# Layer B's sample unit: two heads of 64 rows handled one by one, or above each other in 128 rows

## The chip, the cores and the metric

The kernel runs on one core of a Trainium2 chip. The metric is the device time of one execution in microseconds (us). The core has a matrix engine (TensorE, in the profile PE; its weight loads are PEld), a vector engine (VectorE, DVE), an engine for pointwise functions (ScalarE, ACT), a general one (GpSimd, POOL) and an engine that here only issues transfers (SyncE, SP). Each engine works through its own list of instructions in order and waits on semaphores of the others. TensorE writes to an accumulator memory, PSUM; the other data lie in SBUF, 128 rows (partitions) wide.

## What is computed

One step of a two-layer streaming encoder in float32: 2048 prompt tokens and 64 sample tokens, width 1024, 16 heads of 64 in layer B. Each layer is a gated attention block with a residual. Layer B's band is the own chunk of 64 frames and eight chunks before; the 64 sample tokens see a cache of 256 keys and themselves, so 320 keys, and no mask.

```python
def project(x, norm_g, w_in, q_g, k_g, n_heads, n_kv):
    p = rms_norm(x, norm_g) @ w_in
    q, k, v, gate = jnp.split(p, ...)
    return rms_norm(q, q_g), rms_norm(k, k_g), v, gate      # per head

# attend, layer B: no sinks
s = einsum('bqkgd,bskd->bkgqs', q, k) * dh ** -0.5 + bias
o = einsum('bkgqs,bskd->bqkgd', softmax(s), v)
# layer
y = x + (o * silu(gate)) @ w_out
```

The last rows of keys and values are outputs too.

## The kernel before

Float32 accuracy is made from a fast 32-bit matmul form: every operand is split into a high part and a low part, and a product is the sum of two or three matmuls. Probabilities are split the same way (ph and pl, line 1159), and keys and values carry their low parts in the other half of their rows or columns (KA, KB for the two heads of a prompt pair, KSA, KSB for the sample; VT and VS for values).

Layer B works in eight head pairs (hp). In each it goes through nine units: seven of 256 prompt tokens, then the sample unit of 64 tokens (u == NU), then the eighth prompt unit (order, L220). For each unit there are two kinds of work.

The first is the projection, the "filler" (class Filler, L614): generators that yield after every k-step of a projection, so that it can be cut into slices. Its accumulator pj has two buffers. For the sample tokens high and low parts stand beside each other as 128 columns of the stationary operand, so the accumulator has the sum in two halves of rows, which evacuate (L489) puts together, with ACT for rows 64 to 127 and DVE adding rows 0 to 63. Normalising heads (head_norm, L513), gates (gate), splitting weights and similar jobs go to a background queue (Background, L229): each job has a cost estimate, and each call of share (L272) runs jobs from the head of the queue until max(1.8, a quarter of the queue's cost) is spent. Urgent jobs stand ahead of the others. What share runs is tied, on each engine, behind the last attention instruction there (anchor, L245 and L257 to L265).

The second is attention, in functions that the loop of pipeline (L1201) calls:

- queries (L1044): transposes queries and keys of a unit into the PSUM tile tp, ACT scales the high parts out of it, and two background jobs (low, L1067, cost 1.0 each, urgent) make the low parts from the same tile on DVE, the last of them for KB at L1073. tp has one buffer.
- scores (L1082): score matmuls into sb (L1112, L1113), bias and row minimum on DVE (L1116), exponential and row sum on ACT (L1120), reciprocal, gate times reciprocal on POOL (L1130).
- values (L1137): transposes the probabilities (L596 is the helper that issues every transpose), splits them into ph and pl.
- outputs (L1165): the value product, keys by head width, with the values as stationary operand and the transposed probabilities as moving one (L1190, L1191); for the second head of a pair also the transpose of the gate into tp and finish_pairs (L978), which adds the high and the low half, multiplies with the gate and stores.

A prompt unit has four steps (two heads by two tiles), the sample unit two (its heads). A step of pipeline is: scores, a share, projection up to the first goal, values of the step before, a share, outputs that have come due, projection up to the second goal. queries of the next unit stand at the end of the second step of a prompt unit (QY = 1) and of the first step of the sample unit (QS = 0). TensorE's order is the program's order; on the other engines a scheduler orders the instructions by readiness, within the ties named above. SP issues loads and stores in one queue.

Of the kernel before, what the change touches and what calls it, by code (L numbers as in the profile page):

```python
# [15 lines left out]
P = 128  # L16
# [31 lines left out]
QS = 0  # L48
# [3 lines left out]
def hybrid_encoder_kernel(  # L52
# [296 lines left out]
    def load_act(src, o, T, squares=False, joint=False, lead=None, cache=None, cached=False):  # L349
# [42 lines left out]
        def square(c):  # L392
            def fn():
                s2 = t("res", [P, 2 * OT], 2)[:, : 2 * T].rearrange("p (k s) -> p k s", k=2)
                sq = nc.scalar.activation(s2, raws[c], AF.Square)
                if lead is not None and c > 0:
                    behind(sq.ins, held["wh"])
                part = t("sqr", [P, 2 * T if joint else T], 2)
                nc.vector.tensor_tensor(part[:, :T], s2[:, 0], s2[:, 1], op=ALU.add)
                if x.sum:  # L400
                    nc.vector.tensor_tensor(x.sum[0][:, :T], x.sum[0][:, :T], part[:, :T], op=ALU.add)
                else:
                    x.sum.append(part)
                if joint and c == 3:
                    nc.vector.tensor_copy(x.sum[0][:, T:], x.sum[0][:, :T])
                fetch()
            return fn
# [104 lines left out]

    def head_norm(n, src):  # L513
# [36 lines left out]
    def store_kv(layer, n, kn, v, kdst, vdst):  # L550
        def fn():
            ko = t("ko", [P, 2 * HD], 1)
            nc.gpsimd.tensor_tensor(ko[:n], kn, kgr[:n, layer, :], op=ALU.mult)
            store(kdst, ko[:n])
            store(vdst, v)

        return bg.put(0.1, fn)
# [41 lines left out]

    Q2 = [const([P, 512], f"q2_{i}", F32R) for i in range(2)]  # L600
# [4 lines left out]

    for q in Q2:
        zero(q[64:128])

# [51 lines left out]
    def layer_a():  # L660
# [4 lines left out]
        def add_unit(qd, place, unit):  # L665
# [30 lines left out]
            def take_kv(it, ps):  # L696
                tt, t0, n = it.tile
                last = u == NU
                it.kv = pr = evacuate(0, tt, n, ps, 256, 0)
                kn, v = pr[:n, 0:128], pr[:n, 128:256]  # L700
                split_v(n, v, VS[:, 1] if last else VT[:, tt])
                it.knorm = head_norm(n, kn)
                if last:
                    it.knorm.append(store_kv(0, n, kn, v, ka_s[64:128, :], va_s[64:128, :]))
                elif tt == NT - 1:
                    it.knorm.append(store_kv(0, n, kn, v, ka_p, va_p))
# [283 lines left out]
    def layer_b():  # L990
# [4 lines left out]
        def add_unit(hp, unit):  # L995
# [18 lines left out]
            def gen():  # L1014
# [3 lines left out]
                for e, (tt, t0, n) in enumerate(tiles):  # L1018
                    out = []
                    c = yield from project((tt, t0, n), xc, st.w[hp], 512, out)  # L1020
                    pr = evacuate(1, tt, n, out[0], 512, P, it.gate[:, e])
                    it.prs.append(pr)
                    v, kn = pr[:n, 256:384], pr[:n, 128:256]
                    split_v(n, v, VS[:, 2] if last else VT[:, tt])
# [3 lines left out]
                    if last:  # L1028
                        it.todo.append(store_kv(1, n, kn, v, kb_s[192:256, cols], vb_s[192:256, cols]))
                    elif tt >= NT - 4:  # L1030
                        o = (tt - (NT - 4)) * P
                        it.todo.append(store_kv(1, n, kn, v, kb_p[o : o + P, cols], vb_p[o : o + P, cols]))
# [11 lines left out]
        def queries(it):  # L1044
# [7 lines left out]
            for pr, (tt, t0, n) in zip(it.prs, tiles):  # L1052
                for j in range(2):
                    transpose(tp[:, j * T + t0 : j * T + t0 + n], pr[:n, j * P : (j + 1) * P])
            it.q1 = q1 = t("q1", [P, 2, UT], 2, F32R)
            it.q2 = q2 = low_queries().rearrange("p (h s) -> p h s", h=2)
            if u == NU:
                kd = [a[:, CB : CB + TS] for a in (KSA, KSB)]
            else:
                kd = [a[:, u * UT : (u + 1) * UT] for a in (KA, KB)]  # L1060
            qt = [tp[r, 0:T] for r in halves]
            kt = [tp[r, T : 2 * T] for r in halves]
            for hh, rows in enumerate(halves):
                nc.scalar.activation(q1[rows, hh, :T], qt[hh], AF.Identity, scale=qsc[rows, 1:2])
                nc.scalar.activation(kd[hh][rows], kt[hh], AF.Identity, scale=gk[rows])

            def low(hh, rows):  # L1067
                def fn():
                    nc.vector.scalar_tensor_tensor(
                        q2[rows, hh, :T], qt[hh], qsc[rows, 1:2], q1[rows, hh, :T].bitcast(F32),  # L1070
# [6 lines left out]
                    nc.vector.tensor_copy(q1[halves[1 - hh], hh, :T], q1[rows, hh, :T].bitcast(F32))  # L1077
# [4 lines left out]
        def scores(it, i, h):  # L1082
# [4 lines left out]
            bias = st.bias[hp][h]  # L1087
            last = u == NU
            tt, t0, n = tiles[i]
            if i == 0 and h == 0:  # L1090
# [5 lines left out]
                it.base = 0 if last else max(tt - 4, 0)  # L1096
            if last:
                K, k0, nk = (KSA, KSB)[h], 0, CB + TS
                near, b0 = P, 256
            else:  # L1100
                kt0 = max(tt - 4, 0)
                K, k0, nk = (KA, KB)[h], kt0 * P, (tt - kt0 + 1) * P
                near, b0 = max(nk - 256, 0), 640 - nk
            S = psum_b("sb", 1024, 2)
            rows = halves[h]
            o = 512 - near
            for c0, c1 in ((0, near), (near, nk)):
                if c0 == c1:
                    continue
                kk = K[:, k0 + c0 : k0 + c1]  # L1110
                dst = S[:n, o + c0 : o + c1]
                nc.tensor.matmul(dst, it.q1[:, h, t0 : t0 + n], kk, start=True, stop=False)  # L1112
                nc.tensor.matmul(dst, it.q2[:, h, t0 : t0 + n], kk, start=False, stop=True)  # L1113
            nmh = it.nm[:n, 2 * i + h : 2 * i + h + 1]
            it.p[i, h] = p = t("p", [P, 640], 3)
            mi = nc.vector.tensor_tensor_reduce(  # L1116
                out=p[:n, :nk], in0=S[:n, o : o + nk], in1=bias[:n, b0 : b0 + nk],
                op0=ALU.add, op1=ALU.min, scale=1.0, scalar=3e38, accum_out=nmh,
            )
            ex = nc.scalar.activation(  # L1120
                p[:n, :nk], p[:n, :nk], AF.Exp,
                scale=-1.0, bias=nmh, accum_out=it.sm[:n, 2 * i + h : 2 * i + h + 1],
            )
            bg.anchor(mi, ex)
            if i == len(tiles) - 1 and h == 1:
                w = 2 * len(tiles)
                nc.vector.reciprocal(it.sm[:n, :w], it.sm[:n, :w])
                it.G = G = t("G", [P, 256])
                for e in range(len(tiles)):
# [7 lines left out]
        def values(it, i, h):  # L1137
            u, T, tiles = it.unit
            last = u == NU
# [4 lines left out]
            if last:  # L1144
                sizes, kb = [P, P, TS], 0
            else:
                kt0 = max(tt - 4, 0)
                sizes, kb = [P] * (tt - kt0 + 1), kt0 - it.base
            PT = psum_b("sb", 1024, 2)
            PTv = PT.rearrange("p (c x) -> p c x", x=P)  # L1150
            for c, kn in enumerate(sizes):
                transpose(PTv[:kn, c, :n], it.p[i, h][:n, c * P : c * P + kn])
            full = sum(kn == P for kn in sizes)
            groups = [(0, full, P)]
            if last:
                groups.append((2, 1, TS))
            for c, m, kn in groups:
                bg.anchor(*split_to(
                    it.ph[h][:kn, kb + c : kb + c + m, t0 : t0 + n],
                    it.pl[h][:kn, kb + c : kb + c + m, t0 : t0 + n],  # L1160
                    PTv[:kn, c : c + m, :n],
                ))
            it.sizes = sizes

        def outputs(it, h):  # L1165
            u, T, tiles = it.unit
            last = u == NU
            n = tiles[0][2]
            sizes = it.sizes
            if h == 0:  # L1170
                it.O = psum("o", 512, 1)
            else:
# [3 lines left out]
                gt = gate_t(GT[:, :T].rearrange("p (j s) -> p j s", j=1), T)  # L1176
            mm = []
            if last:
                for c, kn in enumerate(sizes):
                    mm.append((VS[:kn, c, h], c, kn, 0, TS))  # L1180
            else:
                ta, tb = tiles[0][0], tiles[1][0]
                for kt in range(max(tb - 4, 0), ta + 1):
                    mm.append((VT[:, kt, h], kt - it.base, P, 0, UT))
                if ta >= 4:
                    mm.append((VT[:, ta - 4, h], ta - 4 - it.base, P, 0, P))
                mm.append((VT[:, tb, h], tb - it.base, P, P, UT))
            for x, (vt, c, kn, q0, q1_) in enumerate(mm):
                dst = it.O[:, h * T + q0 : h * T + q1_]
                nc.tensor.matmul(dst, vt, it.ph[h][:kn, c, q0:q1_], start=x == 0, stop=False)  # L1190
                nc.tensor.matmul(dst, vt, it.pl[h][:kn, c, q0:q1_], start=False, stop=x == len(mm) - 1)  # L1191
# [9 lines left out]
        def pipeline():  # L1201
# [8 lines left out]
            prev = pend = None  # L1210
            for x, it in enumerate(its):
                heads = [(i, h) for h in range(2) for i in range(len(it.unit[2]))]
                c0 = filler.done
                end, near = c0 + (PACE_B if len(heads) == 4 else PACE_S) * len(heads), 1e9
                if x + 2 < len(its):
                    near = its[x + 2].mark
                    if len(its[x + 1].unit[2]) + len(its[x + 2].unit[2]) < 4:
# [6 lines left out]
                for y, (i, h) in enumerate(heads):  # L1224
# [14 lines left out]
                    if y == (QY if len(heads) == 4 else QS) and x + 1 < len(its):  # L1239
# [4 lines left out]
            filler.to(filler.done + 2.6)  # L1244
            if pend is not None:
                outputs(*pend)
            filler.to(filler.done + 2.6)
            outputs(prev[0], prev[2])
# [210 lines left out]
```

## Time and profile before

| | |
|---|---|
| median of 3 runs | 2306.82 us (2306.8 to 2310.43) |
| the profiled execution's own time | 2309.3 us |
| its span, first to last instruction | 2307.5 us |
| mean granted TensorE clock | 0.998 |
| TensorE busy | 2264.3 us, 98% of the span |
| DVE, ACT, POOL busy | 1562.1, 1435.4, 843.2 us |
| DMA | 379.37 MB, mean 164 GB/s |

The profile is one execution on the chip, taken by the hardware's profiler. The span is its time from the first instruction to the last. L12 is a line of the kernel file; "o<-ph,VS" says that the instruction writes tile o from tiles ph and VS. "128\*64 64x64" beside a matmul gives the stationary operand (rows by columns) and the moving one. "[0.47 <-DVE KB L1073]" says that the engine stood idle for 0.47 us and that the DVE instruction of line 1073 released it. A matmul's length includes its way through the array and overlaps the next one; the distance between two starts is what it costs a busy TensorE.

### The profile page before, as it was taken

Reading aid. Unit: us, or ns where it says so; the run is one execution under the profiler, and the core shown is the slowest. Engines: PE = TensorE matmul, PEld = TensorE weight load, DVE = VectorE, ACT = ScalarE, POOL = GpSimd, SP = SyncE. Lnnn points to the kernel's source line nnn. Section 1 sums busy time; section 2 is a strip of 40 time slices with the busy share of each in tenths; the row PEclk is TensorE's granted clock in tenths of the full one; section 3 lists DMA queues with packets and bytes.
Section 4 is the critical chain, followed back from the end, with each engine's and each line's share of the span. In section 5 each row is a group of like instructions: output and inputs, shape, how many; then the busy total and the mean of one; then the engine's idle time right before and its main releaser. Section 6 shows DMA issues by size and latency. Waiting matters only on the chain.

```text
span 2307.5 us, 42459 instructions
## 1 busy us (share of the span) xinstructions
PE 2264.3 (98%) x13981; PEld 1983.6 (86%) x13981; DVE 1562.1 (68%) x5226; ACT 1435.4 (62%) x3640; POOL 843.2 (37%) x1186
## 2 busy tenths in 40 slices
PE   7999999999999999999999999999999999999999
PEld 6787888888889997888888888888888888888999
DVE  6779988888784446766766767767767677676211
ACT  6778777777774435766656656656656566565321
POOL 5554533333254446432222222222222222224443
PEclk9999999999999999999999999999999999999999
DMA  8846446754446777454444544544445445443665
GB/s 264 261 145 208 162 139 196 229 177 143 150 128 191 215 210 272 156 175 151 138 146 125 157 143 120 158 146 133 145 134 161 127 117 173 125 126 108 194 184 147
DMA packets 232125, 379.37 MB, mean 164 GB/s; under 512 B 24720, under 2 KB 163360, under 8 KB 231872
## 3 DMA queue, kind: packets, MB, share of 16 engines
q1 hardware_dynamic: 231904, 376.65, 53.5%
q8 instruction: 110, 1.80, 0.3%
q14 instruction: 111, 0.91, 0.1%
HBM read 296.13 MB, written 82.08 MB: 164 GB/s over the span
## 4 chain that ended last, share of the span: by engine, by line
PE 82%; DVE 6%; DMA 4%; ACT 4%; issue 2%; POOL 1%; SPq 1%; POOLq 0%; ACTq 0%; DVEq 0%
PE pj L480 13%; PE pj L482 13%; PE pj L481 13%; PE pj L1313 5%; PE pj L1314 5%; PE sb L596 5%; PE pj L1315 5%; PE o L1191 3%; PE o L1190 3%; PE tp L596 3%; PE sb L1112 3%; PE sb L1113 3%; PE sa L596 2%; DMA xraw<-in_x_rows_dram 1%; PE sa L877 1%
## 5 line engine op out<-in xcount | busy, mean ns | idle before, releaser
L480 PE MATMUL pj<-wh,xx 128*128 128x512 f32 (+1 forms) x1648 | 668.3, 406 | 5.3 <-ACT pb L503 4.6
L482 PE MATMUL pj<-wh,xx 128*128 128x512 f32 (+1 forms) x1648 | 638.1, 387 | 0.0
L481 PE MATMUL pj<-wl,xx 128*128 128x512 f32 (+1 forms) x1648 | 635.2, 385 | 0.0
L482 PEld LDWEIGHTS pj<-wh,xx 128*128 128x128 f32 x1648 | 310.8, 189 | 67.2
L480 PEld LDWEIGHTS pj<-wh,xx 128*128 128x128 f32 x1648 | 312.1, 189 | 45.7 <-ACT pb L503 5.3
L481 PEld LDWEIGHTS pj<-wl,xx 128*128 128x128 f32 x1648 | 312.9, 190 | 38.3 <-DVE wl L313 0.2
L384 POOL TENSOR_TENSOR xx<-xraw,xx 128x528 fp32r<-128x528 f32 (+1 forms) x200 | 265.2, 1342 | 200.9 <-ACT xx L383 192.7
L527 POOL TENSOR_TENSOR f<-f,mhalf 128x4 f32<-128x4 f32 (+3 forms) x221 | 227.8, 1031 | 228.4 <-DVE f L523 214.2
L1120 ACT ACTIVATE p<-p,nm 128x640 f32<-128x640 f32 (+5 forms) x272 | 204.3, 751 | 165.9 <-DVE nm L1116 164.1
L1313 PE MATMUL pj<-xx,wh 128*128 128x264 f32 x1024 | 294.0, 287 | 1.6 <-DVE res L1318 1.6
L1314 PE MATMUL pj<-xx,wh 128*128 128x264 f32 x1024 | 291.3, 284 | 0.0
L1315 PE MATMUL pj<-xx,wl 128*128 128x264 f32 x1024 | 289.9, 283 | 0.0
L1116 DVE CUSTOM_DVE_ANT_0 p<-sb,BT 128x640 f32<-128x640 f32 (+5 forms) x272 | 196.8, 724 | 120.1 <-PE sb L1113 116.5
L569 DVE TENSOR_TENSOR pl<-sb,ph 128x640 fp32r<-128x640 f32 (+5 forms) x288 | 196.8, 683 | 117.9 <-ACT ph L568 115.5
L568 ACT CAST ph<-sb 128x640 fp32r<-128x640 f32 (+5 forms) x288 | 167.2, 580 | 128.2 <-PE sb L596 119.9
L986 POOL TENSOR_TENSOR o<-gt,o 128x256 f32<-128x256 f32 (+2 forms) x140 | 107.1, 765 | 374.4 <-issue 156.8
L383 ACT CAST xx<-xraw 128x528 fp32r<-128x528 f32 (+1 forms) x200 | 122.4, 627 | 194.2 <-PE pj L1315 96.9
L1313 PEld LDWEIGHTS pj<-xx,wh 128*128 128x128 f32 x1024 | 192.8, 188 | 2.6 <-DVE res L1318 2.0
L523 DVE CUSTOM_DVE_ANT_0 sq<-pa 128x64 f32<-128x64 f32 (+1 forms) x850 | 171.5, 255 | 34.2 <-ACT pa L503 32.1
L1314 PEld LDWEIGHTS pj<-xx,wh 128*128 128x128 f32 x1024 | 192.5, 188 | 0.2
L1315 PEld LDWEIGHTS pj<-xx,wl 128*128 128x128 f32 x1024 | 192.6, 188 | 0.0
L1318 DVE TENSOR_TENSOR res<-pj,res 128x264 f32<-128x264 f32 x128 | 55.1, 431 | 200.6 <-PE pj L1315 195.6
(196 smaller groups left out, 4810.8 us busy)
## 6 DMA issues: line engine op xcount, KB each, us to landing
xx<-xsb SPq DMA_DIRECT2D x224, 512.0 KB, 4.3
xx<-xsa SPq DMA_DIRECT2D x88, 512.0 KB, 4.8
xraw<-oga SPq DMA_DIRECT2D x64, 264.0 KB, 3.6
xraw<-ogb SPq DMA_DIRECT2D x64, 264.0 KB, 3.3
xsa<-xx SPq DMA_DIRECT2D x32, 512.0 KB, 4.5
wraw<-in_w_in_b_dram SPq DMA_DIRECT2D x64, 256.0 KB, 3.5
xsb<-xx SPq DMA_DIRECT2D x32, 512.0 KB, 4.1
xraw<-in_x_dram SPq DMA_DIRECT2D x40, 256.0 KB, 4.4
```

The costliest lines, as they stand in the source:

```text
L384: nc.gpsimd.tensor_tensor(xl, rv, xh.bitcast(F32), op=ALU.subtract)
L480: nc.tensor.matmul(ps[:n, :C], xh, wh, start=k == 0, stop=False)
L481: nc.tensor.matmul(ps[:n, :C], xh, wl, start=False, stop=False)
L482: nc.tensor.matmul(ps[:n, :C], xl, wh, start=False, stop=k == KC - 1)
L527: nc.gpsimd.tensor_tensor(fv, fv, mhalf[:n, :H], op=ALU.pow)
L569: b = nc.vector.tensor_tensor(dst_lo, src, dst_hi.bitcast(F32), op=ALU.subtract)
L596: nc.tensor.transpose(out, in_, ident[:n, :n])
L1116: mi = nc.vector.tensor_tensor_reduce(out=p[:n, :nk], in0=S[:n, o : o + nk], in1=bias[:n, b0 : b0 + nk], op0=ALU.add, op1=ALU.min, scale=1 ...
L1120: ex = nc.scalar.activation(p[:n, :nk], p[:n, :nk], AF.Exp, scale=-1.0, bias=nmh, accum_out=it.sm[:n, 2 * i + h : 2 * i + h + 1],)
L1313: nc.tensor.matmul(ps[:, :OT], wh, oh, start=k == 0, stop=False)
L1314: nc.tensor.matmul(ps[:, :OT], wh, ol, start=False, stop=False)
L1315: nc.tensor.matmul(ps[:, :OT], wl, oh, start=False, stop=k == KC - 1)
```

## The change

The sample unit of layer B is handled in 128 rows, one head in the upper and one in the lower 64.

- evacuate_sample puts queries of both heads in the upper rows and keys in the lower rows of one 128 x 128 block, values beside them, and the gate with head 0 in the upper and head 1 in the lower rows: five pieces on ACT and five on DVE instead of two and two.
- One transpose brings queries and keys into tp. The queries go into QS, a constant tile of four 128 x 128 blocks (high and low of each head) that is zero outside its head's columns, so that four matmuls add up both heads' scores above each other in 128 rows.
- Bias and minimum stay two DVE instructions (one for each head's rows), the exponential is one of 128 rows. The columns 320 to 383 of the probabilities are zeroed on POOL, and rows 64 to 127 of the last value tile once at the start.
- Three transposes of 128 x 128 and one pair of splits turn the probabilities.
- sample_outputs takes the probabilities as stationary operand and the values of both heads, high and low, as 256 moving columns: six matmuls. The result has tokens in rows; high and low are added, the gate is multiplied without being transposed.
- sample_turned, one step later, transposes the result into tp, scales it by one half on ACT and stores it.
- The sample unit has one step in place of two. Its call of queries for the next unit stands ahead of the step's second goal. What values makes due is kept in a list, todo, of which each step takes one: outputs of the prompt unit before, then sample_outputs, then sample_turned, in the first, second and third step of the eighth prompt unit.
- In layer A, square's partial sums move from the tag sqr, which goes, to the tags G and o1.

```diff
-                part = t("sqr", [P, 2 * T if joint else T], 2)
+                part = t("o1" if x.sum else "G", [P, 256])
...
+    def evacuate_sample(tt, ps, g):
+        a = t("pa", [P, 384], 4)
+        lo, hi = halves
+        pieces = [
+            (a[lo, 0:128], 0), (a[hi, 0:128], 128), (a[lo, 256:384], 256),
+            (g[lo, 0:HD], 384), (g[hi, 0:HD], 384 + HD),
+        ]
+        sc = rr[1][:, tt : tt + 1]
+        for d, c in pieces:
+            nc.scalar.activation(d, ps[hi, c : c + d.shape[1]], AF.Identity, scale=sc[hi])
+        for d, c in pieces:
+            nc.vector.scalar_tensor_tensor(
+                d, ps[lo, c : c + d.shape[1]], sc[lo], d, op0=ALU.mult, op1=ALU.add
+            )
+        return a
...
+    QS = const([P, 4, P], "QS", F32R)
+    zero(QS)
+    zero(VS[64:128, 2])
...
+                    if last:
+                        pr = evacuate_sample(tt, out[0], it.gate[:, e])
+                        it.prs.append(pr)
+                        v, kn = pr[:n, 256:384], pr[n:, 0:128]
+                        split_v(n, v, VS[:, 2])
+                        it.todo += head_norm(P, pr[:, 0:128]) + gate(P, it.gate[:, e, 0:HD])
...
             if u == NU:
+                transpose(tp[:, 0:P], it.prs[0][:, 0:P])
                 kd = [a[:, CB : CB + TS] for a in (KSA, KSB)]
+                q1, q2 = ([QS[:, 2 * e + hh, hh * T : hh * T + T] for hh in range(2)] for e in range(2))
...
+            if u == NU:
+                n, nk, o, w = P, CB + TS, 0, 1
+                nc.gpsimd.memset(p[:, nk : 3 * P], 0.0)
+                for e in range(4):
+                    nc.tensor.matmul(
+                        S[:, :nk], QS[:, 2 * (e % 2) + e // 2], (KSA, KSB)[e // 2], start=e == 0, stop=e == 3
+                    )
+                soft = [(r, st.bias[hp][e][r, b0 : b0 + nk], 0) for e, (r, b0) in enumerate(zip(halves, (256, 320)))]
...
+        def then(it, i, h):
+            if it.unit[0] == NU:
+                return [lambda: sample_outputs(it), lambda: sample_turned(it)]
+            if i == len(it.unit[2]) - 1:
+                return [lambda: outputs(it, h)]
+            return []
+
+        def sample_outputs(it):
+            O = psum("o", 512, 1)
+            for c in range(3):
+                vs = VS[:, c].rearrange("p h d -> p (h d)")
+                nc.tensor.matmul(O[:, 0:256], it.ph[0][:, c, 0:P], vs, start=c == 0, stop=False)
+                nc.tensor.matmul(O[:, 0:256], it.pl[0][:, c, 0:P], vs, start=False, stop=c == 2)
+            it.o = o = t("o1", [P, 256])[:, 0:HD]
+            for hh, r in enumerate(halves):
+                nc.scalar.copy(o[r], O[r, hh * P : hh * P + HD])
+            for hh, r in enumerate(halves):
+                nc.vector.tensor_tensor(o[r], O[r, hh * P + HD : (hh + 1) * P], o[r], op=ALU.add)
+            nc.gpsimd.tensor_tensor(o, it.G[:, 0:HD], o, op=ALU.mult)
+
+        def sample_turned(it):
+            tp = psum("tp", 512, 1)
+            transpose(tp[0:HD, 0:P], it.o)
+            o = t("o1", [P, 256])[:, 0:TS]
+            for hh, r in enumerate(halves):
+                nc.scalar.activation(o[r], tp[0:HD, hh * TS : (hh + 1) * TS], AF.Identity, scale=0.5)
+            store(og[1][:, it.hp, SEQ:TOK], o)
...
+                sample = it.unit[0] == NU
+                heads = [(0, 0)] if sample else [(i, h) for h in range(2) for i in range(2)]
...
-                    nxt = None
+                    nxt = todo.pop(0) if todo else None
                     if prev is not None:
                         values(*prev)
                         bg.share(BL, BP_)
-                        if prev[1] == len(prev[0].unit[2]) - 1:
-                            nxt = prev[0], prev[2]
+                        todo += then(*prev)
                     prev = it, i, h
-                    if pend is not None:
-                        outputs(*pend)
-                    pend = nxt
+                    if nxt is not None:
+                        nxt()
+                    if sample and x + 1 < len(its):
+                        queries(its[x + 1])
+                        near = 1e9
                     goal(2 * y + 2)
```

More of the change, by code (lines that the diff above doesn't have):

```diff
@@ L1076, in fn @@
                     )
[L1077 removed]
+                    nc.vector.tensor_copy(q1[hh][halves[1 - hh]], q1[hh][rows].bitcast(F32))
                 return fn
@@ L1100, in scores @@
             else:
                 kt0 = max(tt - 4, 0)
-                K, k0, nk = (KA, KB)[h], kt0 * P, (tt - kt0 + 1) * P
+                K, k0, nk, w = (KA, KB)[h], kt0 * P, (tt - kt0 + 1) * P, 4
                 near, b0 = max(nk - 256, 0), 640 - nk
[L1104 to L1113, printed above, removed]
@@ L1153, in values @@
[L1153 to L1163, printed above, removed]
+            for c in range(m):
+                transpose(PTv[:, c, :n], it.p[i, h][:n, c * P : (c + 1) * P])
@@ L1243, in pipeline @@
             values(*prev)
[L1244 to L1248, printed above, removed]
+            todo += then(*prev)
+            while todo:
+                filler.to(filler.done + 2.6)
+                todo.pop(0)()
         return pipeline
```

129 lines of the change are left out of this document (68 added, 61 removed).

## The prediction

> **What bounds the kernel now.** I read the page first, then a table of layer B's stretch, then the list of what TensorE waited for, then the timeline of one sample unit.
>
> ```profile
> span 2307.5 us, 42459 instructions
> PE 2264.3 (98%) x13981; PEld 1983.6 (86%) x13981; DVE 1562.1 (68%) x5226; ACT 1435.4 (62%) x3640; POOL 843.2 (37%) x1186
> PE 82%; DVE 6%; DMA 4%; ACT 4%; issue 2%; POOL 1%; SPq 1%; POOLq 0%; ACTq 0%; DVEq 0%
> ```
>
> ```profile
> 1010.00:2133.00 1123.00, 1114.40 (x6596) 959.34 (x6595) 777.25 (x2630) 701.11 (x1773) 312.18 (x487) 1.00 0.46 138
> ```
>
> ```profile
> PE sb L596 <- DVE nm L1116: 4.0, 7, 0.8
> PE tp L596 <- DVE KB L1073: 1.9, 2, 1.4
> ```
>
> TensorE is busy 98% of the span and 82% of the chain of waits. In layer B's stretch (columns: length, then busy time of PE, weight load, DVE, ACT, POOL, then the granted clock) it is busy 1114.4 of 1123 us while DVE and ACT have a third of the time free. The waits from 1000 us on total only a few us. So the change counts by two things alone: TensorE time that it takes out or adds, and waits that it makes TensorE take, since TensorE's order is written by hand and whatever stands behind a waiting matmul waits too. Busy times overlap in the pipeline, so I price a matmul by the distance from its start to the next start.
>
> **What the sample unit costs TensorE.** It stands once in each of the eight head pairs. The second one (columns: start, length, engine, line, tiles, shapes, count):
>
> ```profile
> 1165.68 0.40 PE L482 MATMUL pj<-wh,xx 128*128 128x512 f32 x1
> 1166.01 0.33 PE L596 MATMUL tp<-ident,pa 64*128 64x64 f32 x2
> 1166.28 0.45 PE L1112 MATMUL sb<-KB,q 128*128 128x384 f32 x1
> 1166.56 0.34 PE L1113 MATMUL sb<-KB,q 128*128 128x384 f32 x1
> ...
> 1175.61 0.22 PE L1112 MATMUL sb<-KSA,q 128*64 128x128 f32 x1
> ...
> 1175.91 0.41 PE L480 MATMUL pj<-wh,xx 128*128 128x512 f32 x1
> ...
> 1188.03 0.39 PE L482 MATMUL pj<-wh,xx 128*128 128x512 f32 x1
> 1188.34 0.39 PE L596 MATMUL sb<-ident,p 64*128 64x64 f32 x3
> 1188.67 0.30 PE L1190 MATMUL o<-ph,VS 128*128 128x64 f32 x1
> ...
> 1189.56 0.50 PE L480 MATMUL pj<-wh,xx 128*128 128x512 f32 x1
> 1189.90 0.40 PE L481 MATMUL pj<-wl,xx 128*128 128x512 f32 x1
> ...
> 1193.04 0.71 PE L596 MATMUL sb<-ident,p 128*128 128x128 f32 x5
> 1193.68 0.27 PE L596 MATMUL tp<-ident,G 64*128 64x64 f32 x1
> 1193.88 0.30 PE L1190 MATMUL o<-ph,VS 128*128 128x64 f32 x1
> ```
>
> And what full-height work costs:
>
> ```profile
> 1186.46 0.34 PE L1113 MATMUL sb<-KA,q 128*128 128x384 f32 x1
> 1186.63 0.28 PE L1112 MATMUL sb<-KA,q 128*128 128x256 f32 x1
> 1186.75 0.28 PE L1113 MATMUL sb<-KA,q 128*128 128x256 f32 x1
> ...
> 1198.69 0.71 PE L596 MATMUL sb<-ident,p 128*128 128x128 f32 x5
> 1199.15 0.47 PE L480 MATMUL pj<-wh,xx 128*128 128x512 f32 x1
> 1199.46 0.39 PE L481 MATMUL pj<-wl,xx 128*128 128x512 f32 x1
> ```
>
> A 512-column matmul among its like takes 0.23 us; 384 columns take 0.17, 256 take 0.12. Five full transposes take 0.46, and the matmul behind them starts its successor 0.31 later instead of 0.23: 0.54 in all, 0.11 each. Wherever 64-row work begins or ends, about 0.1 is lost: 1188.03 to 1188.34 is 0.08 over 0.23, 1189.56 to 1189.90 is 0.11 over it.
>
> Before, per sample unit: query transposes 0.10 + 0.27 + 0.11 = 0.48; scores of two heads 0.30 each = 0.60, and 0.02 to get back, 0.62; probability transposes 0.08 + 0.33 = 0.41 for each head, 0.82; value product 1188.67 to 1189.56, 0.89, and 0.11 to get back, 1.00 for each head, 2.00; the gate's transpose 0.20, with the five transposes ahead of it at 0.64 instead of 0.54, 0.30. Sum 4.22 us.
>
> After: one full transpose for queries and keys, 0.11; four score matmuls of 320 columns. That width is not in the trace; it lies between 0.12 and 0.17, and I take 0.147 by columns, 0.59 in all (bounds 0.48 to 0.68), 0.02 to get back; three full transposes 0.33; six value matmuls with 256 moving columns 0.72; the turn of the result 0.11. Sum 1.88 us. Gain 2.34 us a unit, 18.7 us over eight (bounds 18 to 19.6).
>
> **Edits at no cost.** The evacuation goes from two ACT and two DVE instructions to five and five. The nearest ACT row takes 0.36:
>
> ```profile
> 1181.13 0.36 ACT L503 ACTIVATE pb<-pj,rms 128x128 f32<-128x128 f32 x1
> ```
>
> Three more of these and three on DVE are some 2 us. The accumulator they hold is one of two, and the next project on the other lasts 24 matmuls, 5.5 us: hidden; without that cover up to 2 us a unit. One exponential and one pair of splits instead of two and four, and half the norm's squares, relieve ACT and DVE, which bound nothing here. The zeroed tail of the probabilities is a small memset on POOL, ready a whole step before its transpose. The value product moves one step behind its split, as before. SP issues as many loads and stores; the sample's output store leaves a step or so later, and nothing reads it before the output projection. In layer A the partial sums of squares get other buffers. That touches only a start-up wait of 4.2 us (its row is below), and another wait of 1.1 us stands right behind it: bounds 4 us less to 2 us more, I take nothing.
>
> **Where a wait is added.** The turned result needs the tile tp, of which there is one buffer. In the order after the change it stands in the third step of the last prompt unit, behind that step's value transposes. In the second step the same tile was filled with the next head pair's queries (queries, L1044), and it is free when DVE has read it for the last time (low, L1073 on KB). Two projection steps, one score and five transposes lie between. What DVE does in that place today:
>
> ```profile
> 1196.27 0.60 PE L596 MATMUL tp<-ident,pa 128*128 128x128 f32 x4
> ```
>
> ```profile
> 1200.77 0.82 DVE L569 TENSOR_TENSOR pl<-sb,ph 128x640 fp32r<-128x640 f32 x1
> 1201.62 0.49 DVE L1069 SCALAR_TENSOR_TENSOR q<-tp,qsc,q 64x256 fp32r<-64x256 f32 x1
> 1202.13 0.49 DVE L1073 SCALAR_TENSOR_TENSOR KB<-tp,ksc,KB 64x256 fp32r<-64x256 f32 x1
> ```
>
> The background queue explains the order. The share after the scores is worth 1.8. From the second head pair on a tile has just been projected, so the queue holds norm squares 0.6, norm scale 0.4, low half 1.0, second low half 1.0: the second half is left for the share after the value transposes, and is tied behind that step's split on DVE (the 0.82 row). Counting the planner's steps for the new loop gives the same queue at the same place for six head pairs. In the first, no tile has just been projected, and both halves go at once:
>
> ```profile
> 1039.51 0.60 PE L596 MATMUL tp<-ident,pa 128*128 128x128 f32 x4
> ...
> 1041.93 0.71 PE L596 MATMUL sb<-ident,p 128*128 128x128 f32 x5
> ```
>
> ```profile
> 1043.69 0.49 DVE L1073 SCALAR_TENSOR_TENSOR KB<-tp,ksc,KB 64x256 fp32r<-64x256 f32 x1
> ```
>
> How fast TensorE wakes is seen where it meets the same wait today:
>
> ```profile
> 1025.12 0.49 DVE L1073 SCALAR_TENSOR_TENSOR KB<-tp,ksc,KB 64x256 fp32r<-64x256 f32 x1
> ```
>
> ```profile
> 1025.76 0.41 PE L596 MATMUL tp<-ident,G 128*128 128x128 f32 x2 [0.47 <-DVE KB L1073]
> ```
>
> The read ends at 1025.61, TensorE goes on at 1025.76: 0.15. So TensorE would reach the turn at 1198.69 + 0.54 = 1199.23, and may start at 1202.62 + 0.15 = 1202.77: 3.5 us of idle. In the first head pair 1042.47 against 1044.33: 1.9. In the last none, since no queries follow. Together 6 x 3.5 + 1.9 = 22.9 us. Behind the waiting transpose stand all projection matmuls, whose only cover was TensorE itself; ACT and DVE catch up, but they were not late.
>
> Two waits of today, the 1.9 us of the list above, shrink: the next unit's queries now stand half a step earlier with 5 us of projection behind them. The first (0.47) goes, of the last (1.4, where the filler's steps are short) I keep 0.4: 1.5 less. What is late next there is the last unit's first score, on the same reads.
>
> **Sum.** -18.7 + 22.9 - 1.5 = +2.7 us. The profiled execution took 2309.3 us for its span of 2307.5; its median sister runs 2306.82. On the median: 2309.5, which I round to 2310.
>
> **Rivals.** First, the clock, slower. The trace shows one long idle of TensorE and what came of it (in the second fence PEclk is the third number from the end):
>
> ```profile
> 27.45 0.40 PE L482 MATMUL pj<-wh,xx 128*128 128x512 f32 x1
> 32.04 0.58 PE L432 MATMUL o<-ones,sqr 128*128 128x2 f32 x4 [4.19 <-DVE sqr L401]
> ```
>
> ```profile
> 32.60:39.50 6.90, 5.79 (x27) 5.68 (x27) 4.11 (x22) 3.04 (x8) 6.61 (x8) 0.51 0.96 283
> ```
>
> An idle of 4.19 us was followed by 6.9 us at a clock of 0.51, a loss of 3.4 us. Waits up to 1.4 us in layer B left its clock at 1.00. The new 3.5 us stand nearer to the first. If one to six of them bring the half clock, the time is 2313 to 2330; it decides against "no change" from the first one. For the forecast I take none or one, since 3.5 is still short of 4.19.
>
> [...]
>
> Second, the second low half runs in time, faster: if DVE's order puts it ahead of the split, every wait is as in the first head pair, 7 x 1.9 = 13 us, and the time 2299.6. For it speaks that the row of 1043.69 exists; against it the tie to the split, seen in the order of the three DVE rows.
>
> Third, the order of ACT, DVE, POOL and SP is made anew and gives waits of its own, like the seven of up to 0.8 us in the list: 8 us more would be 2318, slower.
>
> Fourth, start-up shortens by its 4 us: 2306, no change to the eye.
>
> **How the numbers follow.** Forecast 0.50, its own range 2304 to 2314; clock 0.20; low half in time 0.13; new waits 0.10; start-up 0.07. About what a measurement can tell from no change is 0.2%, 4.6 us. Of the forecast's half 0.35 lies within it, 0.12 above, 0.03 below. Slower: 0.12 + 0.20 + 0.10 = 0.42; same: 0.35 + 0.05 = 0.40; faster: 0.03 + 0.13 + 0.02 = 0.18. Range 2300 to 2320: below it are the best cases of the second rival, above it four or more half clocks.
>
> **What would show it.** In the list of waits a new line of tp behind KB, seven times, the longest near 3.5 us, 23 us in all. In the groups the 64-row transposes of layer B gone, value rows with 256 moving columns 0.12 apart, score rows of 320 columns about 0.147 apart. PEclk at 1.00 across layer B, or not. It is wrong if that line is absent or half as long, or if the value product in its new form takes more than 0.72.

## The result and the profile after

| | before | after |
|---|---|---|
| median | 2308.62 us (2306.8 to 2311.25, 4 runs) | 2328.21 us (2328.0 to 2330.51, 4 runs) |
| the profiled execution's own time | 2309.3 us | 2330.51 us |
| its span | 2307.5 us | 2328.7 us |
| mean granted TensorE clock | 0.998 | 0.991 |

The ratio of after to before is 1.0086, interval 1.0069 to 1.0104: slower by some 20 us, where 2310 with a range of 2300 to 2320 was predicted. The head of the page after:

```profile
span 2328.7 us, 42202 instructions
PE 2259.3 (97%) x13869; PEld 1984.3 (85%) x13869; DVE 1559.2 (67%) x5194; ACT 1432.8 (62%) x3632; POOL 839.5 (36%) x1196
```

TensorE has 112 matmuls fewer and is busy 5.0 us less (2264.3 before), and yet the span is 21.2 us longer. The answer has two halves, the waits and the clock behind them, and two views show them. First, what TensorE waited for from 1000 us on (engine, tile, line, releaser; then total, times, longest):

```profile
PE tp L609 <- DVE KB L1104: 21.7, 7, 3.4
PE sb L609 <- DVE nm L1150: 4.0, 7, 0.7
PE sb L609 <- DVE pl L582: 3.7, 7, 0.7
PE sb L1147 <- DVE q L1100: 1.4, 1, 1.4
PE o L1243 <- DVE pl L582: 1.2, 5, 0.2
PE sb L1146 <- DVE q L1108: 0.4, 1, 0.4
PE tp L609 <- ACT gt L991: 0.3, 1, 0.3
PE sb L1146 <- DVE KA L1104: 0.2, 1, 0.2
```

The first row is the predicted wait, seven times; the second was there before. The third is new. The 1.4, 0.4 and 0.2 belong to the last unit and stand within 2.5 us of each other. All rows of this list sum to 32.9 us, against 8.5 before: 24.4 more, of which the first row is 21.7 and the others together 2.7.

Second, one of the seven places, the second head pair, in TensorE's timeline (start, length, line, tiles, shapes, idle ahead):

```profile
1195.17 0.71 PE L609 MATMUL sb<-ident,p 128*128 128x128 f32 x5
1199.23 0.40 PE L609 MATMUL tp<-ident,o 128*64 128x128 f32 x1 [3.34 <-DVE KB L1104]
1199.27 0.78 PE L477 MATMUL pj<-wh,xx 128*128 128x512 f32 x1
1199.85 0.63 PE L478 MATMUL pj<-wl,xx 128*128 128x512 f32 x1
1200.27 0.63 PE L479 MATMUL pj<-wh,xx 128*128 128x512 f32 x1
1200.70 0.63 PE L477 MATMUL pj<-wh,xx 128*128 128x512 f32 x1
...
1204.75 0.40 PE L478 MATMUL pj<-wl,xx 128*128 128x512 f32 x1
1204.99 0.39 PE L479 MATMUL pj<-wh,xx 128*128 128x512 f32 x1
```

The turn waits 3.34 us, and the projection matmuls behind it then take 0.63 instead of 0.39 and start 0.43 apart instead of 0.23, until 1204.75. The list counts a wait from the end of the matmul ahead of it. By starts, the turn comes 4.06 us behind the first of the five transposes, where 0.54 would do without a wait: it is delayed by 3.5 us. The seven delays counted so sum to 22.9 us. The same stretch cut into windows (length, busy time of PE, weight load, DVE, ACT, POOL, then the granted clock, DMA share, GB/s):

```profile
1194.51:1197.92 3.41, 1.37 (x9) 0.95 (x7) 3.33 (x15) 2.85 (x7) 1.53 (x2) 1.00 0.62 213
1197.92:1201.34 3.42, 2.11 (x6) 1.76 (x7) 1.63 (x5) 0.43 (x2) 0.00 (x0) 0.50 0.06 14
1201.34:1204.75 3.41, 3.41 (x10) 2.84 (x10) 0.83 (x2) 0.60 (x1) 0.00 (x0) 0.50 0.00 0
1204.75:1210.00 5.25, 5.25 (x34) 4.63 (x33) 1.94 (x12) 2.27 (x8) 0.90 (x3) 1.00 0.10 25
```

The clock goes to 0.50 at 1197.92, while TensorE still waits, stays there for 6.83 us and comes back. The first of these stretches is busy only 1.37 of its 3.41 us. The same happens at every one of the six places with a wait of some 3.3 us, and once more at the last unit's waits. Cut 11 us long, a stretch reads 0.69 when 6.83 us of it ran at half rate and 0.84 when 3.41 us did; the second head pair, the fourth and the last unit:

```profile
1195.00:1206.00 11.00, 7.66 (x31) 6.25 (x30) 5.48 (x18) 3.76 (x11) 2.10 (x4) 0.69 0.23 75
...
1515.00:1526.00 11.00, 7.65 (x42) 6.47 (x41) 5.96 (x19) 4.41 (x11) 2.42 (x5) 0.84 0.21 73
...
2140.00:2151.00 11.00, 9.11 (x57) 8.64 (x58) 6.87 (x13) 2.57 (x7) 2.18 (x3) 0.84 0.47 147
```

Seven stretches at half rate in all, three of 6.83 us and four of 3.41: 34.1 us, of which TensorE was idle for some 3.9. In the other 30.2 a 512-column matmul took 0.427 us from start to start, against 0.232 at full clock: 1.84 times as long and not twice. So some 46% of the 30.2 us, 13.8, were lost.

The span's +21.2 us as a ledger. Layer B's first score starts at 890.01 us instead of 890.90: -0.9. From there on +22.1: the delay of the seven turns +22.9, the other waits +2.7, the half clock +13.8, and the remainder, -17.3, is TensorE's work (waits between that score and 1000 us are counted in it: 2.2 us before, 2.4 after).

### The profile page after: what moved, and what is told of

Its sections match the earlier page's. It is cut to its first block, busy times and chain, and to the rows that moved or that the text cites. A ratio compares the mean times of both kernels' runs of the same rounds, so it can differ in the third digit from the quotient of the medians.

```text
span 2328.7 us, 42202 instructions
## 1 busy us (share of the span) xinstructions
PE 2259.3 (97%) x13869; PEld 1984.3 (85%) x13869; DVE 1559.2 (67%) x5194; ACT 1432.8 (62%) x3632; POOL 839.5 (36%) x1196
## 4 chain that ended last, share of the span: by engine, by line
PE 79%; DVE 8%; DMA 5%; ACT 4%; issue 2%; POOL 1%; SPq 1%; DVEq 0%; ACTq 0%; POOLq 0%
PE pj L477 13%; PE pj L479 12%; PE pj L478 12%; PE pj L1366 5%; PE pj L1367 5%; PE pj L1368 5%; PE sb L609 5%; PE o L1243 3%; PE o L1242 3%; PE tp L609 3%; PE sb L1147 3%; PE sb L1146 3%; DMA xraw<-in_x_rows_dram 2%; PE sa L609 2%; DVE pl L582 1%
## 5 line engine op out<-in xcount | busy, mean ns | idle before, releaser
L582 DVE TENSOR_TENSOR pl<-sb,ph 128x640 fp32r<-128x640 f32 (+4 forms) x264 | 193.3, 732 | 117.0 <-ACT ph L581 114.2
L1002 POOL TENSOR_TENSOR o<-gt,o 128x256 f32<-128x256 f32 (+1 forms) x132 | 102.9, 779 | 386.1 <-DVE o L1001 122.8
L581 ACT CAST ph<-sb 128x640 fp32r<-128x640 f32 (+4 forms) x264 | 163.5, 619 | 116.4 <-PE sb L609 111.1
```

The source lines that it names most:

```text
L582: b = nc.vector.tensor_tensor(dst_lo, src, dst_hi.bitcast(F32), op=ALU.subtract)
```

## The experiments

The kernel before, run beside them on the same chips, had medians of 2308.9 and 2308.91 us. The spans and waits below are those of each kernel's profiled execution. In all sums the measured cost of a matmul is the distance between starts.

### The turn without the shared tile

```
         def sample_outputs(it):
-            O = psum("o", 512, 1)
+            it.O = O = psum("o", 512, 1)
...
         def sample_turned(it):
-            tp = psum("tp", 512, 1)
+            tp = it.O[:, 256:384]
```

The result is turned into a free quarter of the accumulator that it came from; nothing of layer B's queries is touched.

> The turn of the sample's result goes into columns of the accumulator o that the value product left free, so that it no longer needs tp; nothing else differs. Theory (the 21.7 us of waits on tp are the cost, and the half clock is their consequence): the line of tp behind KB goes (21.7 to 0), the clock stays at 1.00 in layer B, and the span falls from 2328.7 by 21.7 and by the 13 to 15 us that I count for the half clock, to 2292 to 2294, faster than before by about 0.6%. Rival A (the clock falls for another reason, such as the 128-row forms): the span falls by 21.7 alone, to 2307, and the half clock stays. Rival B (the wait only moves, to the next use of o, one step later): a new line of o of some 10 to 20 us, span 2305 to 2325.

Measured: 2294.74 us (2292.39 to 2297.15), ratio 0.9938 (0.9923 to 0.9953), span 2292.5. TensorE's timeline at the same place:

```profile
1192.20 0.71 PE L609 MATMUL sb<-ident,p 128*128 128x128 f32 x5
1192.74 0.27 PE L609 MATMUL o<-ident,o 128*64 128x128 f32 x1
1192.77 0.47 PE L477 MATMUL pj<-wh,xx 128*128 128x512 f32 x1
```

Its list of waits from 1000 us on, and its clock up to the last unit and there:

```profile
PE sb L609 <- DVE nm L1150: 4.0, 7, 0.7
PE sb L609 <- DVE pl L582: 3.7, 7, 0.7
PE sb L1147 <- DVE q L1100: 1.4, 1, 1.4
```

```profile
1000.00:2090.00 1090.00, 1080.56 (x6337) 933.62 (x6337) 765.88 (x2586) 690.29 (x1749) 303.99 (x489) 1.00 0.47 141
2103.00:2114.00 11.00, 9.02 (x57) 8.33 (x56) 6.99 (x12) 3.34 (x9) 2.50 (x3) 0.84 0.42 130
```

The transpose of o stands 0.54 us behind the five transposes, as predicted from the rows of before, with no wait. The clock is 1.00 until the last unit, where its 0.44, 1.38 and 0.16 us of waits are left and with them 3.41 us at half rate. So the tile alone made the change slower; without it the change is faster than before. The work is read most cleanly here. From layer B's first score on, the span is 13.0 us shorter than before; its whole list of waits, 11.2 us instead of 8.5, adds 2.7, the half clock at the end 1.6, so TensorE's work is 17.3 us less, 2.2 a unit, as in the changed kernel.

### The wait filled with matmuls

The next three kernels ask how much of the loss is the wait and how much the clock. Here the turn keeps the tile tp, and ahead of it stand 28 matmuls (14 in the first head pair) into the unused half of the accumulator:

```
         def sample_turned(it):
+            if it.hp < 7:
+                for j in range(28 if it.hp else 14):
+                    nc.tensor.matmul(it.O[:, 256:512], QS[:, j % 4], KA[:, 1792:2048], start=True, stop=True)
```

Their results are read by nothing.

> Ahead of the turn TensorE runs 28 added matmuls of 256 columns (14 in the first head pair), 3.3 us of work that nobody reads, into free columns of o. The wait is filled, the time is not given back. Theory (idle brings the half clock): no idle, clock at 1.00 in layer B, span shorter by the 13 to 15 us of the half clock alone, 2314 to 2316. Rival (the clock falls for another reason, or the half clock is not what cost the time): as the changed kernel, 2327 to 2330.

Measured: 2316.86 us (2315.25 to 2318.75), ratio 1.0034 (1.0021 to 1.0047), span 2316.1. TensorE's timeline and layer B's clock:

```profile
1195.23 3.60 PE L1217 MATMUL o<-KA,QS 128*128 128x256 f32 x28
1198.82 0.27 PE L609 MATMUL tp<-ident,o 128*64 128x128 f32 x1
```

```profile
1000.00:2125.00 1125.00, 1115.48 (x6619) 967.21 (x6618) 772.02 (x2602) 696.94 (x1759) 307.34 (x493) 1.00 0.46 138
```

The turn starts about as long after the five transposes as in the changed kernel (4.05 and 4.06 us behind the first of them), and the clock reads 1.00. The same delay without idleness is 12.6 us shorter in span, 12.4 from layer B's first score on, and 11.4 in the median. Counted from the six stretches at half rate it should be 12.2 (30.7 us, idle for 3.9 of them, 46% of the rest). So the half clock alone is worth more than half of the 20 us that the kernel is slower.

### Half of the wait filled

As above with `if 0 < it.hp < 7` and 14 matmuls each, which leaves idle times of 1.7 us.

> The changed kernel with 14 added matmuls (1.65 us, nobody reads them) ahead of the turn in head pairs two to seven, so that seven waits of about 1.7 us are left. In the runs so far every window of 3.41 us with 0.55 or more of it idle was followed by a half clock, and none in layer B with 0.53 or less. An idle of 1.7 us is 0.50 of a window at most. Theory (the threshold is there): no half clock from these waits, span as with the wait filled, 2315 to 2317, although 12 us of idle are back. Rival (a half clock follows any idle near 2 us by chance): two to four half clocks of 1.7 us, 2319 to 2323.

Measured: 2317.72 us (2317.05 to 2317.84), ratio 1.0041 (1.0027 to 1.0055), span 2315.9. TensorE's timeline, its waits, and the clock of the whole rest:

```profile
1196.43 1.92 PE L1217 MATMUL o<-KA,QS 128*128 128x256 f32 x14
...
1200.02 0.27 PE L609 MATMUL tp<-ident,o 128*64 128x128 f32 x1 [1.67 <-DVE KB L1104]
```

```profile
PE tp L609 <- DVE KB L1104: 11.7, 7, 1.7
```

```profile
1000.00:2300.00 1300.00, 1276.90 (x7935) 1128.06 (x7935) 817.33 (x2698) 747.16 (x1850) 383.64 (x555) 1.00 0.48 144
```

Seven waits of 1.7 us, 11.7 in all, and the clock reads 1.00 with them; the span of 2315.9 is the one expected without half clock, and within 0.2 us of that of the wait filled. The idle time need not be zero: here 1.7 us at a time was short enough.

### The turn half a step later

```
+                    late = x > 0 and its[x - 1].unit[0] == NU and y == 2
-                    if nxt is not None:
+                    if nxt is not None and not late:
                         nxt()
...
                     goal(2 * y + 2)
+                    if late:
+                        nxt()
```

The turn stands behind the projection matmuls that it held up before.

> The turn stays in tp, but stands behind the third step's second goal, two projection steps (1.4 us) later. Theory: each wait is 1.4 us shorter, six of 1.9 and one of 0.3, 12 us in all instead of 21.7; and if a half clock needs a window of 3.41 us that is less than about half busy, as the windows ahead of the eight half clocks in the changed kernel are (0.15 to 0.51 not idle), 1.9 us of idle leave 0.44 of a window in the worst phase, so most half clocks go: span 2305 to 2312. Rival (any wait of TensorE this long brings the half clock): six half clocks as now, span 2319.

Measured: 2312.95 us (2311.35 to 2317.01), ratio 1.0019 (1.001 to 1.0029), span 2313.7. Its wait, and two of its six stretches:

```profile
PE tp L609 <- DVE KB L1104: 12.0, 7, 2.0
```

```profile
1196.00:1207.00 11.00, 9.05 (x45) 7.49 (x44) 5.45 (x20) 4.04 (x13) 1.07 (x5) 0.84 0.07 19
...
1511.00:1522.00 11.00, 9.04 (x54) 7.62 (x53) 6.33 (x23) 5.10 (x14) 2.67 (x6) 1.00 0.13 28
```

The wait has the expected size, 12.0 us, its later instances 1.95 us long. The expectation about the clock failed: four of six are still followed by 3.41 us at half rate, though nothing distinguishes them from the other two in length: in the 11 us around them the clock reads 0.84 four times and 1.00 twice. What sets the two apart is not shown.

### The low half ahead of the split

```
-                    bg.share(BL, BP_)
+                    bg.share(2.4 if x and its[x - 1].unit[0] == NU and y == 2 else BL, BP_)
```

The share after the scores of that step is enlarged from 1.8 to 2.4, so that both low halves are issued in it: the second rival of the prediction, made on purpose.

> The share behind the third step's scores of the last prompt unit is worth 2.4 instead of 1.8, so that the second low half of the queries runs there and not behind the value transposes. Theory (the queue decides how long the wait is): all seven waits are like the first, 1.7 to 1.9 us, 12 to 13 us in all, few or no half clocks, span 2304 to 2312. Rival (DVE is late in any case, the queue is not the cause): waits stay at 3.3 us, span 2326 to 2330.

Measured: 2315.22 us (2313.07 to 2318.08), ratio 1.003 (1.0019 to 1.004), span 2311.4. DVE's timeline and TensorE's wait:

```profile
1194.46 0.22 DVE L536 CUSTOM_DVE_ANT_0 sq<-pa 128x64 f32<-128x64 f32 x1
...
1197.25 0.49 DVE L1104 SCALAR_TENSOR_TENSOR KB<-tp,ksc,KB 64x256 fp32r<-64x256 f32 x1
1197.77 0.43 DVE L545 TENSOR_TENSOR pa<-pa,f 128x256 f32<-128x256 f32 x1
```

```profile
PE tp L609 <- DVE KB L1104: 15.3, 7, 2.3
```

In the changed kernel that row of KB starts at 1198.59, behind the 0.82 us of the split; here it starts at 1197.25. So the order on DVE is what sets the wait. But four norm squares of the next tile stand ahead of the lows too, and the six later waits are 2.27 us and not the expected 1.7 to 1.9; two of them are followed by half clock (0.84 in the 11 us around them, 1.00 around the other four). Even with that half in time the tile costs more than the change saves.

### What is left in the new evacuation

The remaining new row, sb behind the split, is read in the first experiment's kernel. DVE's timeline in one head pair, then TensorE's:

```profile
1291.18 1.08 DVE L521 SCALAR_TENSOR_TENSOR pa<-pj,rms,pa 64x128 f32<-64x128 f32 x3 [2.70 <-ACT pb L519]
1292.18 0.56 DVE L521 SCALAR_TENSOR_TENSOR pb<-pj,rms,pb 64x64 f32<-64x64 f32 x2
1292.77 0.82 DVE L582 TENSOR_TENSOR pl<-sb,ph 128x640 fp32r<-128x640 f32 x1
```

```profile
1293.65 0.77 PE L609 MATMUL sb<-ident,p 128*128 128x128 f32 x5 [0.49 <-DVE pl L582]
```

The five pieces stand on DVE ahead of a prompt unit's split, after five on ACT; TensorE waits 0.49 us for that split. In the kernel before, DVE's two pieces at such a place, and no wait:

```profile
1452.60 0.61 DVE L508 SCALAR_TENSOR_TENSOR pa<-pj,rms,pa 64x384 f32<-64x384 f32 x1 [2.02 <-ACT pb L505]
1453.13 0.33 DVE L508 SCALAR_TENSOR_TENSOR pb<-pj,rms,pb 64x128 f32<-64x128 f32 x1
1453.39 0.81 DVE L569 TENSOR_TENSOR pl<-sb,ph 128x640 fp32r<-128x640 f32 x1
```

The experiment, on top of the first one, makes four pieces of five:

```
+        two = ps.rearrange("p (c d x) -> p c d x", d=2, x=P)[:, :, 0]
         pieces = [
-            (a[lo, 0:128], 0), (a[hi, 0:128], 128), (a[lo, 256:384], 256),
-            (g[lo, 0:HD], 384), (g[hi, 0:HD], 384 + HD),
+            (a[lo, 0:256].rearrange("p (c x) -> p c x", x=P), two),
+            (a[hi, 0:128], ps[:, 128:256]),
+            (g[lo, 0:HD], ps[:, 384 : 384 + HD]), (g[hi, 0:HD], ps[:, 384 + HD : 512]),
         ]
```

The two loops over the pieces take the source from this list, and the value is read from its new place.

> The run with the turn in o, and the evacuation of the sample's accumulator in four pieces instead of five on ACT and on DVE (queries and values as one strided piece). With five, DVE writes the attention's pl at 1292.77 behind five pieces of 1.64 us, and the next transposes into sb wait 0.49 us for it, seven times, 3.7 us in all, where before the change there were next to none. Theory (the pieces stand in the way of the split): one piece less on each engine, some 0.3 us each, takes 0.5 to 0.7 off that chain, so most of the 3.7 goes: 0 to 1.5 left, span 2 to 3.5 us shorter than with five. Rival (the split is late for another reason): 3.7 stays.

Measured: 2292.42 us (2290.17 to 2294.82), ratio 0.9932 (0.9918 to 0.9946), span 2293.0. Its row of waits:

```profile
PE sb L609 <- DVE pl L582: 2.0, 7, 0.4
```

One piece fewer on each of the two engines takes 1.7 of the 3.7 us away, which shows that the pieces are a cause; 2.0 are left, more than the 0 to 1.5 expected, and that these come from the other pieces is not shown. In the same list the row of nm falls from 4.0 to 3.6 us, and that of gt grows from 0.3 to 0.9. From layer B's first score (891.06) on, the span is 1.7 us shorter than the first experiment's. The interval overlaps the first experiment's, so the median doesn't separate them.

### The last unit

```
+                if sample and x + 2 >= len(its):
+                    end += 4.2
```

On top of the first experiment, 4.2 us more of the projection is done in the last sample unit, ahead of the last prompt unit's first score.

> The run with the turn in o, and in the last head pair the sample's step gets 4.2 us more of projection, half of it behind the next unit's queries. Theory: the waits of the last unit's first score on those queries, 0.44, 1.38 and 0.16 us, go, and with them the half clock that follows them at 2107 (1.7 us): span 3 to 4 us shorter than 2292.5. Rival: the waits stay because ACT or DVE are late there for another reason, or the added projection runs out of input and waits itself.

Measured: 2293.69 us (2291.8 to 2294.44), ratio 0.9935 (0.9919 to 0.995), span 2292.7. Two rows of its waits, and none of q or of 1.4 any more:

```profile
PE o L609 <- POOL o L1212: 0.4, 1, 0.4
...
PE sb L1146 <- DVE KA L1104: 0.2, 1, 0.2
```

The 0.44 and 1.38 are gone, and the half clock behind them too (1.00 from 2103 to 2114 us, where the first experiment has 0.84), as it should be if the idle times were its cause. A new 0.4 is POOL's, late with the result that is to be turned. By the rows that is 0.44 + 1.38 - 0.4 us of waiting and 1.6 us of half clock less, 3.0 us. The span is no shorter than the first experiment's 2292.5, since layer B's first score starts at 892.42 here and at 888.87 there: start-up differs by more than what is sought. From that score on it is 3.4 us shorter.

### Both together

The last two edits in one kernel.

> Turn in o, four pieces, and the longer last sample step together: if the two gains are apart from each other, 5 to 7 us below the turn in o alone, some 2286 to 2288 in span, 0.8 to 0.9% faster than before.

Measured: 2291.77 us (2289.86 to 2294.85), ratio 0.993 (0.9917 to 0.9942), span 2293.1. The expected span was missed: layer B's first score starts at 893.50, 4.6 us later than in the first experiment, and that is as much as the two edits were to save. From that score on the span is 4.0 us shorter than in the first experiment, where the two edits alone gave 1.7 and 3.4: a little less than their sum, and less than the 5 to 7 expected. The median is the lowest of all, 17 us below the kernel before, and its interval overlaps those of the three kernels that it is made from.

## Why the prediction was wrong

Its sum, term by term: -18.7 + 22.9 - 1.5 = +2.7 us predicted, +21.2 us in the span.

| term | predicted | measured |
|---|---|---|
| TensorE's work | -18.7 | -17.3 (first experiment: -17.3) |
| delay of the turn by tp | +22.9 | +22.9 |
| other waits from 1000 us on | -1.5 | +2.7 |
| half clock | 0 | +13.8 |
| up to layer B's first score | 0 | -0.9 |

**The step that failed** is the sentence "For the forecast I take none or one, since 3.5 is still short of 4.19." All six waits of 3.3 us brought the half clock, 12.2 us, and the last unit's waits a seventh, 1.6. It was named as the first rival with 2313 to 2330, and given 0.20. The comparison was wrong in kind: the rows of before gave one idle time that was followed by half clock (4.19) and one that was not (1.4). An idle time between two such rows should have had a cost from both ends, 0 to 20 us by the prediction's own price, and the range its upper end. Instead the sum took the lower one.

The price of 3.4 us for one half clock was too high: it took the clock of 0.51 for twice the time and counted idle time with it, and the seven here cost 1.3 to 2.8 us each. That the rival's 2330 for six of them lies so near the measured 2328 is therefore partly luck: the price put it 8.2 us too high, and the seventh half clock, the other waits, the work and the start-up came out 6.3 us higher than the sum had them.

The rows of before had more to compare than the length of the wait, 4.19 us. The half clock there begins at 32.68, and of the 3.41 us ahead of it, from 29.27, TensorE was busy for 0.58 us: idle by 0.83 of them. Of the 3.41 us ahead of each of the six half clocks in the changed kernel it was idle by 0.60 to 0.85.

**Edits at no cost** failed by its cover. It named the accumulator that the pieces hold, and that was hidden, as argued: no wait of TensorE for pj stands in the lists of layer B. But the pieces also stand in ACT's and DVE's own order ahead of the next split of the attention, for which TensorE waits seven times, 3.7 us in all. "Without that cover up to 2 us a unit" looked at the wrong resource; 0.5 us a unit came through.

**The two old waits**: "The first (0.47) goes" was right. "of the last (1.4, where the filler's steps are short) I keep 0.4" was not: "what is late next there is the last unit's first score" was right as a name, but it waits 0.44 + 1.38 + 0.16 = 2.0 us and brings a half clock. Both sides had moved: the score comes 4.3 us behind the transposes of its queries instead of 7.6, and the read of tp for KA ends 6.6 us behind them instead of 3.3.

**What was right.** The wait's place, releaser and size: seven times, first 1.7 and the others 3.34, 21.7 us in the list of waits, and 1.9 and 3.5, 22.9 in all, by starts, which is how the prediction counted. So the reading of the background queue held, and the tie to the split did too: with the low half put ahead of it the wait went from 3.34 to 2.27. The new matmuls: 320-column scores 0.146 apart (0.147), 256-column value matmuls 0.117 (0.12), the turn behind the transposes at once. The work saved is 17.3 instead of 18.7, just under the lower bound of 18; which of its parts is short by 0.18 us a unit was not measured by itself. The start-up was not tried alone: between runs layer B's first score varies from 888.9 to 893.5 us, more than that rival's 4 us.

## What to carry to other kernels

When a step moves on the engine that bounds the kernel, look up who read its single-buffered tile last; a tile already at hand may make the wait vanish, and here that alone turned a loss of 20 us into a gain of 14. Price an idle time of TensorE twice, once as the wait and once as the clock behind it: here each of six waits of 3.34 us was followed by half clock, by my estimate (46% of the busy time in it) 1.3 to 2.8 us more, and filling them, or all but 1.7 us of each, saved this second part (spans of 2316.1 and 2315.9 us instead of 2328.7). When an evacuation is split into more instructions, ask not only who needs its accumulator but what stands behind it in the same engine's order.

## What the runs showed of the hardware

In the traces of the kernel before and of the changed one the stretches at 0.50 last 3.41 or 6.83 us, apart from one at the end of each trace, and within a trace any two changes between 1.00 and 0.50 lie a whole multiple of 3.413 us apart (1197.92 and 1358.35 are 47 of them). The changed kernel's trace, cut into windows of 3.41 us at such multiples, gives from 1000 us up to 2324 us, with transposes as busy, for windows at full clock:

| window from | idle share of it | what followed |
|---|---|---|
| 1194.51 | 0.60 | 6.83 us at 0.50 |
| 1354.94 | 0.75 | 6.83 us at 0.50 |
| 1515.36 | 0.85 | 3.41 us at 0.50 |
| 1675.79 | 0.66 | 3.41 us at 0.50 |
| 1832.80 | 0.75 | 6.83 us at 0.50 |
| 1993.23 | 0.80 | 3.41 us at 0.50 |
| 2140.00 | 0.55 | 3.41 us at 0.50 |
| 1037.50 | 0.50 | 1.00 |
| all others | 0.32 or less | 1.00 |

In the kernel before, the most idle of these windows from 1000 to 2300 us has 0.41, and the clock stays at 1.00.

By the length of the turn's wait:

| kernel | wait | waits | followed by half clock |
|---|---|---|---|
| half of the wait filled | 1.7 us | 7 | the clock reads 1.00 from 1000 to 2300 us |
| turn half a step later | 1.95 us | 6 | 4 |
| low half ahead of the split | 2.27 us | 6 | 2 |
| changed kernel | 3.34 us | 6 | 6 |

So the length of a wait alone does not sort the runs between 1.95 and 2.27 us; what else does is not shown.

In the changed kernel the half clock stayed for a second 3.41 us three times, where TensorE was idle by 0.23 to 0.38 of the first, and did not four times, where it was idle by 0.17, 0.13 and twice not at all. While it lasted, a 512-column matmul took 0.427 us from start to start instead of 0.232, a 264-column one 0.220 instead of 0.122, a transpose 0.213 instead of 0.109: 1.8 to almost 2 times as long. In the first 300 us, the changed kernel's window from 27.15 was idle by 0.49 and half clock followed; its window from 225.12 was idle by 0.52 and none did. What else counts there was not settled.
